# Plain float32 V blocks of the first layer: every sixth block, or 18 blocks beside the last chunk's weights

## The chip, the cores and the metric

The kernel runs on one core of a Trainium2 chip. The metric is device time in microseconds of one launch, given as the median of several runs. The core has a matrix engine (PE, with its weight loads as PEld), a vector engine (DVE), an activation engine (ACT), GpSimd (POOL), a queue engine for transfers (SP), and 16 DMA engines that all queues share.

## What is computed

Two layers of a diffusion backbone over 512 latent tokens and 256 context tokens of width 1024. The part that the change touches is the expert retrieval (PEER) at the end of each layer: every token picks, for 8 heads, the best 16 of 16,384 experts, and

```
act = jax.nn.gelu(jnp.einsum('td,thkd->thk', xb, u_tab[eid]))
return jnp.einsum('thk,thkd->td', gate * act, v_tab[eid])
```

`u_tab` and `v_tab` have 16,384 rows of 1024 float32 each. A token needs 128 rows of each.

## The kernel before

The retrieval is done in two ways at once. For some tiles of 128 tokens the rows that the tokens chose are **gathered**: POOL issues an indirect DMA (L1123) of 128 rows (512 KB) into one of five `grow` buffers, and DVE multiplies it in with one instruction on 128x1024, at L1134 for U (a dot product) and at L1147 for V (an accumulation). In the first layer both context tiles and latent tile 3 are gathered, 128 gathers each for U and V. The other 384 latent tokens go the **dense** way, in `peer_x`: all 128 experts of a block are applied to all 384 tokens, and the activations of experts that a token did not choose are multiplied by zero.

`peer_x` has 128 U blocks and 128 V blocks of 128 experts. A U block loads 512 KB, splits it into a high and a low float32r part, and multiplies it with the tokens in 24 matmuls (tile `pst`); ACT writes the gelu into a slot of the ring `PA`/`PB`, which has R = nA + nB = 64 slots (L1233). A call of `weights(c, i)`, here a round of weights, builds for 8 tokens the gates of one chunk c of blocks from one-hot matrices (DVE: two `o` tiles and `og`; in odd rounds ACT makes the second `o`), multiplies them on PE (16 matmuls, tile `pwt`) and scales the slots by them (DVE, two instructions at L1270). The first layer has three chunks, of 36, 46 and 46 blocks, with 48 rounds each. A V block loads 512 KB into a `uv` tile, of which there are two. A **split** V block then makes `uvh` (ACT, L113) and `uvl` (DVE, L114) from it, and `wh` (ACT) and `wl` (DVE) from the slot, and multiplies in 18 float32r matmuls into the accumulators `dacc`; the `uv` tile is free after the splits. A **plain** V block (the first branch of `vblock`, L1275) has no splits: 6 float32 matmuls, recorded as 12, read the `uv` tile and the slot itself, and the tile is free only after the last of them.

The loop runs m from -nB to 127: the rounds that are due at m, then V block m, then U block m + 64 while there is one. So U ends with m = 63, the second chunk's rounds are due from m = 18 to 35, and the last chunk's from m = 64 to 81. V block 82 is the first to read a slot that the last chunk's rounds scale.

What order the instructions of each engine stand in is settled when the kernel is built: a scheduler gives every engine a fixed list, by the priorities of `prio` (lower numbers first: `peer_x` has 3, the gathers have 6 and fill what the scheduler takes for gaps). On the chip each engine works its list off in order, so a DVE instruction that waits for a gather holds everything behind it. After `peer_x` the second layer's front (L464) follows, which first needs the new latent rows and later those of the context; the last gathers belong to a context tile.

Of the kernel before, what the change touches and what calls it, by code (L numbers as in the profile page):

```python
# [71 lines left out]
class Kern:  # L72
# [101 lines left out]
    def schedule(self):  # L174
        a = self.a
        with ExitStack() as er:
# [19 lines left out]
            with self.banks("x0", "left", w=2, S=2) as ps:  # L196
                with ExitStack() as e:
                    with self.prio(3):
                        pr = e.enter_context(self.banks("x0b", "right", w=2))
                        st = self.front(e, ps, pr, 0, 0, 3, split=False)  # L200
                        ex, keep = ExitStack(), ExitStack()
                        rn = self.back(ps, pr, 0, 0, st, ex, keep=keep)
# [4 lines left out]
                self.gtile_v(0, 1, 0, gc[0])  # L207
                self.gtile_u(0, gc[1])
            with self.prio(3):
                gx, ex = self.peer_x(0, 384, 6, 31, 33, (36, 46, 46), ex, rn)  # L210
            with self.prio(6):
                self.gtile_u(0, gx[3])
                self.gtile_v(0, 0, 3, gx[3])
# [7 lines left out]
                with self.prio(4):  # L221
                    self.back(ps, pr, 1, 0, st, None, (2, 6))
            with self.prio(5):
                gx, _ = self.peer_x(1, 320, 0, 32, 46, (44, 42, 42), (ex,))
            with self.prio(6):
                for i in sorted(gx, reverse=True):
                    self.gtile_u(1, gx[i])
# [953 lines left out]
        nc.sync.dma_start(self.out[t * 128:(t + 1) * 128, :][rows], res[rows])  # L1181


    def peer_x(self, l, T, vn, nA, nB, widths, done, rn=None):

# [5 lines left out]
        R = nA + nB  # L1193
        cuts = [sum(widths[:i]) for i in range(len(widths) + 1)]
        wid = max(widths)
        with ExitStack() as es:
            dn = es.enter_context(self.pool(f"dn{l}"))
            P = [dn.tile([128, nA, T], F32, name="PA")]
# [73 lines left out]

            def vblock(i, sp):
                r0 = l * NEXP + i * 128
                if vn and i % vn == vn - 1:  # L1275
                    raw = dn.tile([128, D], F32, name="uv", bufs=2 + l)
                    nc.sync.dma_start(raw, a["peer_v"][r0:r0 + 128, :])
                    v, w = [raw], [slot(i)]
                else:
                    raw, v = block("v", a["peer_v"][r0:r0 + 128, :])  # L1280
                    w = [sp.tile([128, nd * 128], F32R, name=n, bufs=2) for n in ("wh", "wl")]
                    self.split(*w, slot(i)[:, :nd * 128])
                vh = [[x[:, h * 512:(h + 1) * 512] for x in v] for h in range(2)]
                for t in range(nd):
                    for h in range(2):
                        self.mm([acc[t][:, h * 512:(h + 1) * 512]], [[x[:, t * 128:(t + 1) * 128] for x in w]],
                                [vh[h]], i == 0, i == 127)
                if half:
                    for h in range(2):
                        nc.tensor.matmul(acc[nd][h * 64:(h + 1) * 64], slot(i)[:, nd * 128:T],  # L1290
                                         raw[:, h * 512:(h + 1) * 512], start=(i == 0), stop=(i == 127))
# [174 lines left out]
```

## Time and profile before

| | |
|---|---|
| runs shown, us | 4254.28, 4270.21, 4272.61 (median 4270.21) |
| profiled execution, us | 4259.61, span of its instructions 4257.7 |
| mean granted clock of PE | 0.939 of full speed |
| busy in the span | PE 87%, DVE 82%, PEld 66%, ACT 45%, POOL 36% |
| DMA | 1063.74 MB, mean 250 GB/s |

A share of the span is an average over stages that have different limits. The layer's dense part is therefore cut into stretches below, at instructions that stand in both kernels.

### The profile page before, as it was taken

The page shows a single profiled execution, that of the slowest core. Times are in us where ns is not written, and L with a number is a line of the kernel's source. Part 1 is how long each engine was busy: PE and PEld are TensorE (multiplying, and loading weights), DVE is VectorE, ACT ScalarE, POOL GpSimd, SP SyncE. Part 2 cuts the span into 40 slices and gives each one's busy share as a digit, 9 for nine tenths or more (in the row PEclk, how much of TensorE's full clock was granted, in tenths as well). Part 3 has the DMA queues.
Part 4 walks back from the last instruction along what each step waited for, and adds up shares of the span by engine and source line. Part 5 has one row for each costly group of instructions (what it writes and reads, how often), then busy time and mean ns, then how long its engine had stood idle before and what let it go on. Part 6 is the DMA issues. An engine that isn't in the chain of part 4 may idle for free.

```text
span 4257.7 us, 63783 instructions
## 1 busy us (share of the span) xinstructions
PE 3709.5 (87%) x22514; PEld 2804.8 (66%) x22514; DVE 3508.1 (82%) x7449; ACT 1902.7 (45%) x3719; POOL 1524.0 (36%) x1225
## 2 busy tenths in 40 slices
PE   6887988967989999988968979888888999999997
PEld 3645544557878878877756656447888877776654
DVE  5746988889899989988898875754898988898988
ACT  4555243523247426622552244633334755555732
POOL 0000345642344564366436620000126345553243
PEclk7998998979989999999989989998999999999999
DMA  6655687885768897799879952242359888888697
GB/s 204 203 178 183 214 307 244 300 288 185 250 226 266 307 363 268 243 361 348 292 233 332 348 181 87 84 142 100 138 180 352 270 296 296 294 299 277 227 352 274
DMA packets 305634, 1063.74 MB, mean 250 GB/s; under 512 B 35756, under 2 KB 42624, under 8 KB 305314
## 3 DMA queue, kind: packets, MB, share of 16 engines
q0 software_dynamic: 165888, 604.05, 40.8%
q1 hardware_dynamic: 139426, 455.61, 30.7%
q8 instruction: 177, 2.90, 0.3%
q14 instruction: 143, 1.17, 0.1%
HBM read 1042.69 MB, written 16.84 MB: 249 GB/s over the span
## 4 chain that ended last, share of the span: by engine, by line
PE 32%; DMA 21%; DVE 19%; issue 16%; POOL 6%; ACT 5%; SPq 0%; POOLq 0%; DVEq 0%; ACTq 0%
PE pst L121 7%; POOL grow L1123 6%; PE dacc L121 6%; DMA grow<-in_peer_u_dram,eid 6%; DMA grow<-in_peer_v_dram,eid 5%; DMA uv<-in_peer_v_dram 4%; PE pwin L121 4%; DMA uv<-in_peer_ut_dram 3%; DVE uvl L114 3%; DVE acc L1147 3%; DVE acc L1134 2%; PE ppq L121 2%; DMA wmod<-in_w_mod_dram 2%; PE pwo L121 1%; PE fp L414 1%
## 5 line engine op out<-in xcount | busy, mean ns | idle before, releaser
L1123 POOL DMA_INDIRECT grow<-in_peer_u_dram,eid x576 | 749.6, 1301 | 1166.6 <-DVE acc L1134 591.8
L1123 POOL DMA_INDIRECT grow<-in_peer_v_dram,eid x576 | 766.8, 1331 | 748.0 <-DVE acc L1147 604.4
L121 PE MATMUL pst<-dhT,uvh 128*128 128x384 f32 (+1 forms) x4096 | 998.6, 328 | 0.0
L113 ACT CAST uvh<-uv 128x1024 fp32r<-128x1024 f32 x491 | 512.9, 1045 | 699.7 <-DMA uv<-in_peer_v_dram 422.4
L121 PE MATMUL pst<-dhT,uvl 128*128 128x384 f32 (+1 forms) x2048 | 695.2, 339 | 115.5 <-DVE uvl L114 83.9
L1147 DVE SCALAR_TENSOR_TENSOR acc<-grow,gate,acc 128x1024 f32<-128x1024 f32 x571 | 732.9, 1283 | 49.9 <-DMA grow<-in_peer_v_dram,eid 42.9
L1134 DVE SCALAR_TENSOR_TENSOR acc<-grow,ghx 128x1024 f32<-128x1024 f32 x576 | 704.4, 1223 | 73.4 <-DMA grow<-in_peer_u_dram,eid 68.4
L121 PEld LDWEIGHTS pst<-dhT,uvh 128*128 128x128 f32 x4096 | 730.6, 192 | 2.8 <-issue 1.2
L114 DVE TENSOR_TENSOR uvl<-uv,uvh 128x1024 fp32r<-128x1024 f32 x491 | 599.5, 1222 | 154.8 <-ACT uvh L113 152.1
L121 PEld LDWEIGHTS pst<-dhT,uvl 128*128 128x128 f32 x2048 | 394.2, 192 | 218.2 <-DVE uvl L114 163.5
L121 PE MATMUL dacc<-uvh,wl 128*128 128x512 f32 x1154 | 482.0, 418 | 40.1 <-ACT uvh L113 21.3
L121 PE MATMUL dacc<-uvl,wh 128*128 128x512 f32 x1154 | 468.8, 406 | 25.7 <-DVE uvl L114 25.4
L121 PE MATMUL dacc<-uvh,wh 128*128 128x512 f32 x1154 | 462.9, 401 | 0.0
L1263 ACT ACTIVATE o<-iota,di2n 128x128 f16<-128x128 f16 x1056 | 325.2, 389 | 27.6 <-PE pwt L1267 27.4
L121 PEld LDWEIGHTS dacc<-uvh,wl 128*128 128x128 f32 x1154 | 220.6, 191 | 130.3 <-ACT uvh L113 37.0
L121 PEld LDWEIGHTS dacc<-uvl,wh 128*128 128x128 f32 x1154 | 221.1, 192 | 84.5 <-DVE uvl L114 40.2
L121 PEld LDWEIGHTS dacc<-uvh,wh 128*128 128x128 f32 x1154 | 221.2, 192 | 47.9
L1267 PEld LDWEIGHTS <-o 128*128 128x128 f16 x4224 | 126.4, 97 | 104.3 <-issue 31.1
L1233 ACT ACTIVATE PA<-pst 128x320 f32<-128x320 f32 (+1 forms) x126 | 58.4, 463 | 290.4 <-PE pst L121 290.3
L1267 PE MATMUL pwt<-og,o 128*128 128x46 f16 (+3 forms) x4224 | 152.3, 183 | 37.1 <-DVE og L1253 29.7
L1233 ACT ACTIVATE PB<-pst 128x384 f32<-128x384 f32 (+1 forms) x130 | 60.0, 462 | 218.2 <-PE pst L121 218.1
L256 POOL MEMSET rmod<- 128x512 f32 (+1 forms) x8 | 3.3, 416 | 421.1 <-PE ptmod L282 171.8
(403 smaller groups left out, 6104.5 us busy)
## 6 DMA issues: line engine op xcount, KB each, us to landing
uv<-in_peer_ut_dram SPq DMA_DIRECT2D x256, 512.0 KB
uv<-in_peer_v_dram SPq DMA_DIRECT2D x256, 512.0 KB
wmod<-in_w_mod_dram SPq DMA_DIRECT2D x96, 512.0 KB
wpq<-in_peer_wq_dram SPq DMA_DIRECT2D x48, 512.0 KB
w_in<-in_w_in_dram SPq DMA_DIRECT2D x72, 256.0 KB
w_in<-in_w_in_dram SPq DMA_DIRECT2D x18, 512.0 KB
grow<-in_peer_u_dram,eid POOLq DMA_INDIRECT x576, 6.6
grow<-in_peer_v_dram,eid POOLq DMA_INDIRECT x576, 6.8
```

Of the source, the lines that this page charges most:

```text
L113: self.nc.scalar.copy(hi, src)
L114: self.nc.vector.tensor_tensor(lo, src, hi.bitcast(F32), op=ALU.subtract)
L121: self.nc.tensor.matmul(p, w[i], x[j], start=start and n == 0, stop=stop and n == len(passes) - 1)
L256: nc.gpsimd.memset(r, 0.0)
L414: self.nc.tensor.matmul(p, w, x, start=(i == 0), stop=(i == len(pairs) - 1))
L1123: self.nc.gpsimd.indirect_dma_start(out=r, out_offset=None, in_=self.a[table], in_offset=bass.IndirectOffsetOnAxis(ap=eid[:, j:j + 1], axi ...
L1134: nc.vector.scalar_tensor_tensor(junk, r, 1.0, hx, op0=ALU.mult, op1=ALU.mult, accum_out=dot[:, j:j + 1])
L1147: nc.vector.scalar_tensor_tensor(acc, r, w[:, j:j + 1], acc, op0=ALU.mult, op1=ALU.add)
L1233: nc.scalar.activation(slot(i), p, AF.Gelu_apprx_tanh)
L1263: nc.scalar.activation(o2[:, q], self.iota, AF.Abs, bias=i2n[:, t, k * NC + q:k * NC + q + 1])
L1267: nc.tensor.matmul(p[:, q, :], o2[:, q, :], og[:, g, q, :], start=(g == 0), stop=(g == 1))
```

## The change

The argument vn (every vn-th V block plain) goes; in the first layer the plain blocks are now those from 128 - R to the start of the last chunk, which is 64 to 81: 18 blocks in a row. Before they were 5, 11, ... 125: 21 blocks. The second layer had none and has none.

```diff
-                gx, ex = self.peer_x(0, 384, 6, 31, 33, (36, 46, 46), ex, rn)
+                gx, ex = self.peer_x(0, 384, 31, 33, (36, 46, 46), ex, rn)
...
-                gx, _ = self.peer_x(1, 320, 0, 32, 46, (44, 42, 42), (ex,))
+                gx, _ = self.peer_x(1, 320, 32, 46, (44, 42, 42), (ex,))
...
-    def peer_x(self, l, T, vn, nA, nB, widths, done, rn=None):
+    def peer_x(self, l, T, nA, nB, widths, done, rn=None):
...
         wid = max(widths)
+
+        plain = range(128 - R, cuts[-2]) if l == 0 else ()
...
             def vblock(i, sp):
                 r0 = l * NEXP + i * 128
-                if vn and i % vn == vn - 1:
+                if i in plain:
```

The lists of the engines move with it. POOL's list of gathers keeps its order. On DVE they stand elsewhere between the other instructions. Here is DVE's list early among the last chunk's rounds (V blocks 64 to 81), before: `og`, `o` and the two at L1270 belong to the rounds, `uvl` and `wl` to split V blocks, L1147 is a gather.

```order
L1253 TENSOR_TENSOR og<-o_18387,diT 128x736
L1147 SCALAR_TENSOR_TENSOR acc<-grow,gate,acc 128x1024
L1270 SCALAR_TENSOR_TENSOR PA<-pwt,PA 128x13x8
L1270 SCALAR_TENSOR_TENSOR PB<-pwt,PB 128x33x8
L1248 TENSOR_TENSOR o_18448<-iota,diT 128x368
L1259 TENSOR_TENSOR o_18510<-iota,diT 128x1024
L1253 TENSOR_TENSOR og<-o_18448,diT 128x736
L114 TENSOR_TENSOR uvl<-uv,uvh 128x1024
L1270 SCALAR_TENSOR_TENSOR PA<-pwt,PA 128x13x8
L1270 SCALAR_TENSOR_TENSOR PB<-pwt,PB 128x33x8
L1248 TENSOR_TENSOR o_18473<-iota,diT 128x368
L114 TENSOR_TENSOR wl<-PA,wh 128x384
```

The same place of the changed kernel:

```order
L1255 TENSOR_TENSOR og<-o_18567,diT 128x736
L1147 SCALAR_TENSOR_TENSOR acc<-grow,gate,acc 128x1024
L1272 SCALAR_TENSOR_TENSOR PA<-pwt,PA 128x13x8
L1272 SCALAR_TENSOR_TENSOR PB<-pwt,PB 128x33x8
L1250 TENSOR_TENSOR o_18608<-iota,diT 128x368
L1261 TENSOR_TENSOR o_18670<-iota,diT 128x1024
L1255 TENSOR_TENSOR og<-o_18608,diT 128x736
L1147 SCALAR_TENSOR_TENSOR acc<-grow,gate,acc 128x1024
L1272 SCALAR_TENSOR_TENSOR PA<-pwt,PA 128x13x8
L1272 SCALAR_TENSOR_TENSOR PB<-pwt,PB 128x33x8
L1250 TENSOR_TENSOR o_18633<-iota,diT 128x368
L1147 SCALAR_TENSOR_TENSOR acc<-grow,gate,acc 128x1024
```

Where `uvl` and `wl` stood, there are now gathers. The second place is DVE's list just behind the last round, where V block 82 begins, before (x2 and so on: equal instructions in a row):

```order
L114 TENSOR_TENSOR wl<-PA,wh 128x384 x2
L1147 SCALAR_TENSOR_TENSOR acc<-grow,gate,acc 128x1024 x4
L114 TENSOR_TENSOR uvl<-uv,uvh 128x1024
L114 TENSOR_TENSOR wl<-PA,wh 128x384
L1147 SCALAR_TENSOR_TENSOR acc<-grow,gate,acc 128x1024 x6
L114 TENSOR_TENSOR uvl<-uv,uvh 128x1024
L114 TENSOR_TENSOR wl<-PA,wh 128x384
L1147 SCALAR_TENSOR_TENSOR acc<-grow,gate,acc 128x1024 x2
```

and in the changed kernel:

```order
L114 TENSOR_TENSOR wl<-PA,wh 128x384 x2
L1147 SCALAR_TENSOR_TENSOR acc<-grow,gate,acc 128x1024 x4
L114 TENSOR_TENSOR uvl<-uv,uvh 128x1024
L114 TENSOR_TENSOR wl<-PA,wh 128x384
L1147 SCALAR_TENSOR_TENSOR acc<-grow,gate,acc 128x1024 x2
L114 TENSOR_TENSOR uvl<-uv,uvh 128x1024
L114 TENSOR_TENSOR wl<-PA,wh 128x384
L1147 SCALAR_TENSOR_TENSOR acc<-grow,gate,acc 128x1024 x2
```

Two gathers now stand between any two V blocks; before there were 4 to 6 around a plain one. The third place is DVE's list where the last gathers meet the second layer's front (`hT`, `xn`, `w_inl`, `hc` are the front's, L1156 and L1172 end the gathered context tile), before:

```order
L1147 SCALAR_TENSOR_TENSOR acc<-grow,gate,acc 128x1024
L114 TENSOR_TENSOR hT_22355<-hraw,hT_22354 128x4x128 x2
L107 SCALAR_TENSOR_TENSOR nrt<-nry,nrm 128x1
L1156 TENSOR_TENSOR acc<-acc,grow 128x1024
L108 SCALAR_TENSOR_TENSOR nry<-nrt,nry 128x1
L1172 TENSOR_TENSOR grow<-grow,acc 128x1024
L423 TENSOR_SCALAR xn<-xr,nry 128x1024
L114 TENSOR_TENSOR w_inl<-w_in,w_inh 128x512
```

and in the changed kernel:

```order
L1147 SCALAR_TENSOR_TENSOR acc<-grow,gate,acc 128x1024
L114 TENSOR_TENSOR hT_22415<-hraw,hT_22414 128x4x128 x2
L107 SCALAR_TENSOR_TENSOR nrt<-nry,nrm 128x1
L1147 SCALAR_TENSOR_TENSOR acc<-grow,gate,acc 128x1024
L108 SCALAR_TENSOR_TENSOR nry<-nrt,nry 128x1
L1147 SCALAR_TENSOR_TENSOR acc<-grow,gate,acc 128x1024
L423 TENSOR_SCALAR xn<-xr,nry 128x1024
L1147 SCALAR_TENSOR_TENSOR acc<-grow,gate,acc 128x1024
L114 TENSOR_TENSOR w_inl<-w_in,w_inh 128x512
```

Ten gathers more stand behind the dense part than before. Counted over the whole list of DVE between instructions that both kernels have, the gathers (L1134 and L1147), the splits `uvl` and `wl`, and the rounds (`og`) move as follows. S1 runs from the first `wl` to the 51st `og` of the layer (the first of the second chunk behind two that stand ahead), S2 from there to the 98th, S3 to the 99th, S4 to the 144th and last, S5 to the first instruction that reads `dacc` (L1332), S6 to the last gather of the context tile.

| stretch | V blocks, about | gathers before, after | `uvl` | `wl` | `og` |
|---|---|---|---|---|---|
| S1 | 0 to 19 | 90, 83 | 33, 36 | 16, 19 | 1, 1 |
| S2 | 20 to 36 | 42, 36 | 32, 35 | 14, 17 | 47, 47 |
| S3 | 37 to 63 | 135, 129 | 53, 56 | 25, 27 | 1, 1 |
| S4 | 64 to 81 | 30, 56 | 16, 2 | 13, 0 | 45, 45 |
| S5 | 82 to 127 | 111, 94 | 36, 44 | 38, 46 | 0, 0 |
| S6 | behind V | 16, 26 | 0, 0 | 0, 0 | 0, 0 |

On SP the loads keep their order; three small transfers for the end of the layer (`PA<-rows`, two `PA<-xsd`) stand one or two V loads earlier. Behind the front of the second layer the lists are the same.

## Rows read from the trace of the kernel before

**Rows 1.** The page's busy times: engine, busy us, share of the span, instructions.

```profile
PE 3709.5 (87%) x22514; PEld 2804.8 (66%) x22514; DVE 3508.1 (82%) x7449; ACT 1902.7 (45%) x3719; POOL 1524.0 (36%) x1225
```

**Rows 2.** Windows S1 to S6: PE, PEld, DVE, ACT, POOL busy; clock, DMA share, GB/s.

```profile
1433.50:1619.60 186.10, 169.67 (x792) 139.18 (x790) 157.06 (x237) 54.23 (x79) 122.59 (x90) 0.97 0.97 356
1619.60:1790.40 170.80, 169.81 (x1438) 143.11 (x1439) 165.20 (x342) 122.25 (x269) 57.60 (x43) 1.00 0.73 240
1790.40:2077.50 287.10, 258.89 (x1217) 214.24 (x1216) 243.89 (x261) 81.25 (x114) 182.14 (x136) 0.98 0.95 351
2077.50:2216.00 138.50, 105.39 (x1022) 75.49 (x1020) 132.95 (x265) 98.42 (x231) 29.62 (x31) 0.88 0.67 216
2216.00:2456.10 240.10, 214.69 (x795) 150.87 (x796) 200.16 (x189) 54.22 (x74) 148.92 (x112) 0.96 0.93 336
2456.10:2495.50 39.40, 10.01 (x38) 7.06 (x37) 39.26 (x65) 21.79 (x50) 15.38 (x17) 0.53 0.80 277
```

**Rows 3.** L1147 in S5, and L1134 in S1: count, shortest, median, longest ns.

```profile
L1147 DVE SCALAR_TENSOR_TENSOR acc<-grow,gate,acc x111: 1272/1285/1341, 2216.5 to 2454.9; 128x1024 f32<-128x1024 f32 x111
...
L1134 DVE SCALAR_TENSOR_TENSOR acc<-grow,ghx x90: 1217/1224/1228, 1435.3 to 1617.4; 128x1024 f32<-128x1024 f32 x90
```

**Rows 4.** PE's timeline around a plain block of S5: start, us, instruction, count.

```profile
2254.81 5.31 PE L121 MATMUL dacc<-uv,PA 128*128 128x512 f32 x12
...
2260.42 0.40 PE L121 MATMUL dacc<-uvh,wh 128*128 128x512 f32 x1
...
2263.94 0.40 PE L121 MATMUL dacc<-uvh,wh 128*128 128x512 f32 x1
```

**Rows 5.** DVE's timeline late in S4: two rounds and three gathers.

```profile
2190.65 0.54 DVE L1253 TENSOR_TENSOR og<-o,diT 128x736 f16<-128x736 f16 x1
2191.11 1.28 DVE L1147 SCALAR_TENSOR_TENSOR acc<-grow,gate,acc 128x1024 f32<-128x1024 f32 x1
2192.30 0.26 DVE L1270 SCALAR_TENSOR_TENSOR PA<-pwt,PA 128x104 f32<-128x104 f32 x1
...
2194.13 1.28 DVE L1147 SCALAR_TENSOR_TENSOR acc<-grow,gate,acc 128x1024 f32<-128x1024 f32 x1
2195.32 0.26 DVE L1270 SCALAR_TENSOR_TENSOR PA<-pwt,PA 128x104 f32<-128x104 f32 x1
...
2197.29 0.54 DVE L1253 TENSOR_TENSOR og<-o,diT 128x736 f16<-128x736 f16 x1
```

**Rows 6.** DVE's timeline in S5: a split V block between gathers.

```profile
2340.30 1.21 DVE L114 TENSOR_TENSOR uvl<-uv,uvh 128x1024 fp32r<-128x1024 f32 x1
2341.43 0.55 DVE L114 TENSOR_TENSOR wl<-PB,wh 128x384 fp32r<-128x384 f32 x1
2341.90 2.60 DVE L1147 SCALAR_TENSOR_TENSOR acc<-grow,gate,acc 128x1024 f32<-128x1024 f32 x2
```

**Rows 7.** Windows of S4 in two parts, and the first of S5, as in 2.

```profile
2077.50:2182.00 104.50, 97.74 (x862) 68.97 (x860) 98.98 (x202) 79.87 (x185) 17.24 (x19) 0.98 0.65 212
2182.00:2216.00 34.00, 7.64 (x161) 6.52 (x160) 33.97 (x64) 18.55 (x46) 12.38 (x12) 0.55 0.72 229
2216.00:2223.00 7.00, 3.80 (x23) 3.12 (x24) 6.49 (x10) 0.92 (x2) 4.24 (x4) 0.50 0.91 289
```

**Rows 8.** SP's and ACT's timelines in S1: a V load and its cast.

```profile
1484.51 0.33 SPq L1224 DMA_DIRECT2D uv<-in_peer_v_dram  x1
...
1490.11 1.04 ACT L113 CAST uvh<-uv 128x1024 fp32r<-128x1024 f32 x1 [6.49 <-DMA uv<-in_peer_v_dram]
```

**Rows 9.** Waits in S5: who for whom, us in all, times, longest us.

```profile
ACT uvh L113 <- DMA uv<-in_peer_v_dram: 145.0, 32, 8.8
```

**Rows 10.** Window behind S6, the second layer's front, as in 2.

```profile
2495.50:2530.00 34.50, 34.50 (x145) 28.43 (x144) 21.40 (x36) 10.79 (x20) 0.67 (x10) 0.94 0.34 109
```

## The prediction

> **What bounds the kernel now.** The page is read first [rows 1]: PE 87% and DVE 82% busy, no engine full, which says only that the stages differ. So the dense part of the first layer is cut into windows S1 to S6, at DVE instructions that both kernels have [rows 2]. The reader is to see that two kinds of stretch alternate. In S1, S3 and S5 the DMA engines are the full ones: share 0.97, 0.95 and 0.93 at 356, 351 and 336 GB/s, while PE and DVE are busy for 83 to 91% of the time. In S2 it is PE (169.8 of 170.8 us) and in S4 DVE (133.0 of 138.5 us), and there the DMA engines move only 240 and 216 GB/s. S6 is DVE again (39.3 of 39.4 us).
>
> That S1, S3 and S5 are paced by bytes can be checked by counting. One block load and one gather are both 512 KB, 0.524 MB. S1 moves 356 GB/s x 186.1 us = 66.3 MB, that is 126 transfers, and by the table of the change it holds 90 gathers and about 36 block loads. S3 moves 100.8 MB = 192 transfers (135 gathers, some 56 loads), S5 80.7 MB = 154 (111 gathers, some 43 loads). The gathers' counts in the trace are those of the list [rows 3]. So in these three stretches a gather costs its bytes: 0.524 MB / 0.356 = 1.47 us in S1, 1.49 in S3, 1.56 in S5, whatever it costs DVE.
>
> **The prices of the engines.** A plain block is 12 records in 5.31 us. The split block behind it has a matmul every (2263.94 - 2260.42)/15 = 0.235 us, so 18 of them take 17 x 0.235 + 0.40 = 4.39 us, both counted to the end of the last one [rows 4]. Plain costs PE 0.92 us more. On DVE the two rounds and three gathers from 2190.65 to 2197.29 take 6.64 us without a gap; a gather holds the engine 2192.30 - 2191.11 = 1.19 us, so a round takes (6.64 - 3.57)/2 = 1.53 us on average [rows 5]. A split block's `uvl` takes 2341.43 - 2340.30 = 1.13 us and its `wl` 0.47 [rows 6]: plain spares DVE 1.60 us.
>
> **The change part by part.** Three plain blocks fewer save PE 2.8 us and cost DVE 4.8 us in all, which is little. What counts is where the list now puts 424 gathers that are the same in number: 36 leave S1 to S3 and S5 (7, 6, 6 and 17), 26 of them go into S4 and 10 into S6.
>
> S1 loses 7 gathers: 7 x 1.47 = 10 us. Cover for more isn't there: PE is at 91%, and three splits more on DVE (4.8 us) stand against seven gathers less (8.3 us). If DMA did not pace it, the gain is PE's three plain blocks alone, 2.8 us; that is one bound, and 13 us with the DMA share at 1.0 the other. I take -10.
>
> S2 is PE's own: three plain blocks become split, 3 x 0.92 = 2.8 us; the 6 gathers that leave cost nothing there. -3, between 0 and -6 (DVE, at 97%, loses 7.1 us and gains 4.8).
>
> S3 loses 6 gathers, 9 us by bytes, between 3.7 us (four plain blocks on PE) and 13. I take -9.
>
> S4 is where the splits go and the gathers come. By the prices it held 45 x 1.53 + 30 x 1.19 + 16 x 1.13 + 13 x 0.47 = 128.7 us of DVE work in 138.5 us, 93%. In the new list it is 45 x 1.53 + 56 x 1.19 + 2 x 1.13 = 137.8 us; at the same 93% that is 148 us, +10. The 24 us that the splits spare are more than spent by 26 gathers (31 us). There is less air than before, though. In the part up to the last plain block (the first window) PE was busy 97.7 of 104.5 us [rows 7]; 15 blocks at 0.92 us make it 111.5 us of the 114 that DVE takes there (148 less the 34 of the second window), and a round goes from DVE to PE and back, with about three plain matmuls queued ahead of it on PE. Each hitch on one engine then reaches the other. I take +14, between +4 (DVE without a gap) and +30. The loads don't set it: from issue to cast a V load took 5.6 us at a DMA share of 0.97 [rows 8]; with two tiles, each held for a load and for a block of 5.3 us and its rounds' matmuls, a block could come about every 6 us, and DVE lets one through every 114/18 = 6.3. On ACT 15 casts of `uvh` and `wh` go, and it wasn't full (98 of 138.5 us).
>
> S5 gets 8 splits more and 17 gathers less. DVE's balance is 8 x 1.60 - 17 x 1.19 = -7 us, PE's 8 x -0.92 = -7 us, so both stay under the end; the bytes fall by 8.9 MB, at the rate held 26 us. The bounds: 15 us if the turn-around of the two `uv` tiles rather than bytes sets part of it (ACT's casts wait 145 us in all for V loads there [rows 9]), 38 us if the stretch came up to the 356 GB/s of S1. I take -26.
>
> On this the Trainium skill has a rule (DMA: Bandwidth & Descriptors, section "Where 436 GB/s comes from"): transfers from HBM to SBUF are bound at about 358 GB/s for each core. S1's 356 and S3's 351 GB/s [rows 2] agree with it. By that figure S5 would take (80.7 - 8.9) MB / 0.358 = 201 us, 39 less, and the sum would be 13 us lower than mine; an estimate from that page, which I do not use as the end of a range.
>
> S6 and what follows: ten gathers more stand among the first matmuls of the second layer. They are 10 x 1.19 = 12 us of DVE work, and the first 34.5 us there left DVE 13.1 us idle while PE was busy throughout [rows 10]. Most of it hides; a `w_inl` that stands behind a late gather holds PE. +3, between 0 and +10. SP's list moves three small transfers by one or two V loads, each behind blocks that the two `uv` tiles make it wait for anyway: nothing. From there on the lists are equal, so the rest keeps its time.
>
> **Sum.** -10 - 3 - 9 + 14 - 26 + 3 = -31 us. Against the profiled execution of 4259.6 us that is 4228.6. That execution lies 10.6 us under the median of the runs shown, and the four executions have their middle at 4264.9; from there the sum gives 4234, and that is my number.
>
> **The rivals.** *S4 eats it.* Plain blocks, rounds and gathers need 97% of PE and 93% of DVE at once in the first window. If the two lose a tenth to each other, S4 costs +30 and S5, with its tiles turning slowly, gives only 20: -9 in all, 4256, no change that can be told. For it speaks how close the two sums lie; against it that DVE kept 93% with PE at 94% already [rows 7]. Chance 0.27, with the milder mixtures of it.
>
> *S5 fills up.* With plain blocks gone the loads come evenly, and S5 reaches S1's 356 GB/s: 38 us in place of 26, 4222. S5 is the stretch with the most room below S1's rate. Chance 0.18.
>
> *PE slows down in S4.* The granted clock was 0.98 while PE was 94% busy, and 0.55 in the 34 us in which DVE alone worked off the last rounds; V block 82 then began at 0.50, the 1.2 GHz level [rows 7]. In the new list PE waits before each round's matmuls. If these waits took the clock to 1.2 GHz for the whole of the first window, 111.5 us of PE work become 223, S4 grows by some 110 us and the kernel by 65, to 4330. It decides from about half of that window at 1.2 GHz: 4234 + 55 lies near 0.5% above the old median. Against it: PE would be about as busy there as it was, and slow matmuls fill its gaps themselves. Chance 0.05. The Trainium skill (TensorE: Matmul & The Clock Gate, section "What's actually happening") has the low level as the default, released by activity; that goes with the 0.55 and 0.50 of the rows, and it is the rule by which this case would come.
>
> *The change does nothing of this* is excluded by the lists: the gathers stand where the table says.
>
> **How the numbers follow.** The forecast itself, -20 to -50 us, has 0.50; with the others that makes 1. The limit of what counts as a change, 0.5% of 4270, is 21 us, about what a measurement of this kernel can tell from none. The forecast and a full S5 make it faster, less a tenth of the forecast that lies near the limit: 0.63. S4's case and that tenth make no change: 0.32. The clock's case is the slower one: 0.05. The ends of the terms add up to -66 and +19 us, which no case reaches with all terms at once; eight in ten lie between -59 and -5 from the 4265, so 4206 to 4260.
>
> **What the profile will show.** Right: S1, S3 and S5 shorter by 10, 9 and 26 us at rates within 2 or 3% of before, S4 at about 152 us with DVE still over 93% busy and DMA up from 216 towards 290 GB/s, the front of the second layer with PE hardly waiting. Wrong: S4 over 165 us, with rounds on DVE waiting for `pwt` or gathers; S5 above 225 us, or its GB/s below 320; S1 or S3 unchanged although their gathers left; a clock under 0.9 in the first 100 us of S4.

## The result, and the profile after

The changed kernel takes 4217.44 us (median of six runs, 4202.68 to 4229.7), the kernel before 4271.41 us beside it (six runs): a ratio of 0.9876, 95% interval 0.9848 to 0.9904, that is 41 to 65 us less. The profiled execution of the changed kernel is the longest of its six, 4229.7 us, and 30 us shorter than that of before.

The page's busy line, as in [rows 1], tells as little as before:

```profile
PE 3702.5 (88%) x22532; PEld 2806.4 (66%) x22532; DVE 3509.9 (83%) x7455; ACT 1908.9 (45%) x3725; POOL 1543.7 (37%) x1225
```

The windows S1 to S6 of the changed kernel answer to [rows 2] (PE, PEld, DVE, ACT, POOL busy; clock, DMA share, GB/s). The last row is a stretch that is needed below, called the end: from the first read of `dacc` to the last matmul into `pwin`, a tile of the second layer's front. Behind it the lists are the same.

```profile
1431.45:1607.30 175.85, 162.36 (x808) 138.58 (x807) 152.92 (x229) 58.29 (x85) 122.12 (x83) 1.00 0.96 358
1607.30:1776.40 169.10, 168.49 (x1456) 147.49 (x1457) 162.83 (x335) 125.68 (x276) 48.44 (x37) 0.99 0.69 226
1776.40:2051.50 275.10, 252.81 (x1244) 216.06 (x1242) 239.97 (x272) 88.28 (x123) 177.26 (x129) 1.00 0.96 353
2051.50:2197.80 146.30, 117.06 (x928) 60.48 (x928) 142.19 (x264) 79.02 (x200) 56.90 (x57) 0.88 0.86 301
2197.80:2409.40 211.60, 199.65 (x836) 155.00 (x837) 191.38 (x189) 65.29 (x90) 142.93 (x94) 0.98 0.94 337
2409.40:2473.10 63.70, 34.84 (x137) 26.71 (x136) 61.88 (x92) 27.69 (x60) 31.38 (x33) 0.71 0.82 276
2409.40:2580.30 170.90, 135.88 (x634) 110.92 (x632) 103.89 (x162) 64.68 (x133) 32.55 (x47) 0.87 0.46 149
```

The end of the kernel before:

```profile
2456.10:2622.30 166.20, 131.81 (x626) 109.08 (x625) 92.70 (x152) 64.70 (x133) 16.95 (x37) 0.87 0.37 123
```

S1, S3 and S5 are shorter by 10.2, 12.0 and 28.5 us at rates of 358, 353 and 337 GB/s (356, 351 and 336 before), S2 by 1.7. S4 is 7.8 us longer with DVE at 97%, the end 4.7. To the last `pwin` matmul that makes 42 us (2622.3 - 2580.3). The rest of the kernel took 1635.4 us before and 1647.6 now (spans 4257.7 and 4227.9), although its lists are the same. One of the experiments (x_some_before) has the lists of before and took 1654.0 there (4269.6 - 2449.1 - 166.5): this part scatters by 10 to 20 us between executions, and so the two profiles differ by only 30 us, where the medians show 54.

S4 in parts, as in [rows 7]:

```profile
2051.50:2155.00 103.50, 101.03 (x705) 49.86 (x706) 99.61 (x187) 56.05 (x144) 41.58 (x42) 0.98 0.88 313
2155.00:2197.80 42.80, 16.03 (x224) 10.62 (x222) 42.58 (x78) 22.97 (x56) 15.32 (x16) 0.62 0.82 273
2197.80:2205.00 7.20, 3.99 (x24) 3.23 (x25) 7.13 (x11) 0.92 (x2) 4.76 (x4) 0.50 0.83 270
```

In the first 103.5 us PE is busy for 97.6% and DVE for 96.2% at a clock of 0.98. In S5 the waits of [rows 9] read

```profile
ACT uvh L113 <- DMA uv<-in_peer_v_dram: 114.8, 36, 5.5
```

Four waits more than before, but 30 us less in all, and the longest is 5.5 us in place of 8.8.

### The profile page after: what moved, and what is told of

It reads as the page before. It is cut to its first block, busy times and chain, and to the rows that moved or that the text cites. A ratio compares the mean times of both kernels' runs of the same rounds, so it can differ in the third digit from the quotient of the medians.

```text
span 4227.9 us, 63819 instructions
## 1 busy us (share of the span) xinstructions
PE 3702.5 (88%) x22532; PEld 2806.4 (66%) x22532; DVE 3509.9 (83%) x7455; ACT 1908.9 (45%) x3725; POOL 1543.7 (37%) x1225
## 4 chain that ended last, share of the span: by engine, by line
PE 35%; DMA 21%; DVE 18%; issue 15%; POOL 7%; ACT 5%; SPq 0%; POOLq 0%; DVEq 0%; ACTq 0%
PE pst L121 8%; PE dacc L121 7%; DMA grow<-in_peer_u_dram,eid 7%; POOL grow L1123 7%; DMA uv<-in_peer_v_dram 5%; PE pwin L121 4%; DMA uv<-in_peer_ut_dram 3%; DMA grow<-in_peer_v_dram,eid 3%; DVE uvl L114 2%; PE ppq L121 2%; DVE acc L1147 2%; DVE acc L1134 2%; PE fp L414 2%; PE pwo L121 2%; DMA wmod<-in_w_mod_dram 2%
## 5 line engine op out<-in xcount | busy, mean ns | idle before, releaser
L1123 POOL DMA_INDIRECT grow<-in_peer_v_dram,eid x576 | 782.1, 1358 | 700.5 <-DVE acc L1147 553.8
L1134 DVE SCALAR_TENSOR_TENSOR acc<-grow,ghx 128x1024 f32<-128x1024 f32 x576 | 703.1, 1221 | 76.1 <-DMA grow<-in_peer_u_dram,eid 71.1
L1147 DVE SCALAR_TENSOR_TENSOR acc<-grow,gate,acc 128x1024 f32<-128x1024 f32 x571 | 731.1, 1280 | 33.5 <-DMA grow<-in_peer_v_dram,eid 27.0
L256 POOL MEMSET rmod<- 128x512 f32 (+1 forms) x8 | 3.3, 417 | 419.3 <-PE ptmod L282 169.2
```

What stands on the lines that cost most here:

```text
L256: nc.gpsimd.memset(r, 0.0)
L1123: self.nc.gpsimd.indirect_dma_start(out=r, out_offset=None, in_=self.a[table], in_offset=bass.IndirectOffsetOnAxis(ap=eid[:, j:j + 1], axi ...
L1134: nc.vector.scalar_tensor_tensor(junk, r, 1.0, hx, op0=ALU.mult, op1=ALU.mult, accum_out=dot[:, j:j + 1])
L1147: nc.vector.scalar_tensor_tensor(acc, r, w[:, j:j + 1], acc, op0=ALU.mult, op1=ALU.add)
```

## The experiments

**Theory 1** is the prediction's: S1, S3 and S5 are paced by bytes, and the gain is that gathers leave them for S4. **Theory 2**, the rival: the plain blocks themselves cost time in S1, S3 and S5, and the gain is that they left. From the fifth run on it has a sharper form: a plain block keeps one of the two `uv` tiles through its 5.3 us of matmuls. All edits are to the changed kernel unless said otherwise; each run was timed beside the kernel before.

The stretches of all profiled executions, us, and the medians, with the median of before in the same comparison:

| kernel | S1 | S2 | S3 | S4 | S5 | end | median | before | ratio (95%) |
|---|---|---|---|---|---|---|---|---|---|
| before | 186.1 | 170.8 | 287.1 | 138.5 | 240.1 | 166.2 | | | |
| changed | 175.9 | 169.1 | 275.1 | 146.3 | 211.6 | 170.9 | 4217.4 | 4271.4 | 0.9876 (0.9848 to 0.9904) |
| x_none | 174.1 | 167.5 | 273.3 | 128.0 | 214.9 | 213.9 | 4250.5 | 4271.2 | 0.9944 (0.9921 to 0.9967) |
| x_both | 187.2 | 169.7 | 294.7 | 150.7 | 237.1 | 156.1 | 4264.4 | 4271.2 | 0.9984 (0.9968 to 1.0001) |
| x_small_before | 158.5 | 169.6 | 248.3 | 136.0 | 205.3 | 166.6 | 4099.8 | 4271.2 | 0.9597 (0.9579 to 0.9616) |
| x_small_after | 155.1 | 168.0 | 242.7 | 140.3 | 197.2 | 169.0 | 4090.1 | 4271.2 | 0.9573 (0.9551 to 0.9596) |
| x_some_before | 182.1 | 170.9 | 289.7 | 139.1 | 237.1 | 166.5 | 4268.0 | 4275.2 | 0.9982 (0.9961 to 1.0003) |
| x_some_after | 169.2 | 167.6 | 270.9 | 147.6 | 207.6 | 169.9 | 4222.1 | 4275.2 | 0.9875 (0.9846 to 0.9904) |
| x_s3 | 174.0 | 167.5 | 322.6 | 129.2 | 212.7 | 173.7 | 4247.0 | 4275.2 | 0.9927 (0.9902 to 0.9951) |
| x_s2s4 | 171.5 | 210.5 | 271.8 | 150.9 | 211.1 | 157.0 | 4245.7 | 4275.2 | 0.9924 (0.9901 to 0.9947) |
| x_hold | 179.9 | 172.3 | 283.8 | 149.2 | 230.2 | 169.3 | 4259.6 | 4265.4 | 0.9980 (0.9962 to 0.9999) |
| x_pe | 176.5 | 172.0 | 270.7 | 152.3 | 219.6 | 167.0 | 4228.0 | 4265.4 | 0.9904 (0.9880 to 0.9928) |
| x_own | 186.0 | 169.9 | 287.6 | 139.3 | 235.3 | 167.3 | 4266.9 | 4265.4 | 0.9995 (0.9978 to 1.0012) |
| x_own_s5 | 172.5 | 167.6 | 277.2 | 150.9 | 235.1 | 166.4 | 4237.0 | 4265.4 | 0.9921 (0.9895 to 0.9946) |

Stretches of kernels with the same lists there differ by up to 5 us (S1 is 171.5 to 175.9 in the changed kernel, x_s2s4 and x_own_s5, S4 146.3 to 150.9 in the changed kernel, x_some_after and x_own_s5), so a difference of that size in one stretch tells nothing.

### x_none and x_both: the change's two halves

```diff
# x_none
-        plain = range(128 - R, cuts[-2]) if l == 0 else ()
+        plain = () if l == 0 else ()
# x_both
-        plain = range(128 - R, cuts[-2]) if l == 0 else ()
+        plain = (*range(128 - R, cuts[-2]), *range(5, 64, 6), *range(83, 128, 6)) if l == 0 else ()
```

Expected of x_none: 

> No plain block at all. Theory 1 (the gain is gathers that leave the byte-bound S1, S3 and S5 for room that the plain blocks open in S4): in this kernel's list S4 holds 22 gathers (56 in the changed kernel), S3 127 (129), S5 91 (94), and 65 stand behind the V blocks in S6 (26). Against the 4217 us of the changed kernel: S4 -14 us (124 us of DVE work in place of 138, at the same 0.94 busy), S3 -3, S5 -5, and 39 more gathers in S6 cost between +18 us (0.47 us each, as the ten of the change did) and +57 us (their bytes): 4213 to 4252, middle 4233; S1 and S5 keep the lengths that they have in the changed kernel. Theory 2 (the gain is the removal of plain blocks from S1, S3 and S5 itself, by PE's 0.92 us and the uv tile's longer hold; the 18 beside the weights add nothing): 4200 or less, since S4 gives its 14 us back and nothing is lost.

Expected of x_both: 

> The old sixth blocks outside 64 to 81 stay plain, and 64 to 81 are plain too: 36 plain blocks. Theory 1: S4 holds 56 gathers, S5 99 (before 111), S3 137 (135), S6 none (16). Against the kernel before: S4 +8 us as in the changed kernel, S5 12 x 1.56 = -19, S3 +3, S6 and the second layer's front 16 x 0.47 = -7: about -15 us, 4256, with S1 as long as before (186 us). Theory 2: no plain block has left S1, S3 or S5, so nothing is gained and S4 costs 8 us more: 4279.

The removal alone gave 21 us, the addition alone 7 (its interval, 14 to 0 us, reaches none at all), the two together 54. x_none's S1, its S4 and S5, and its end (as two answers of the windows):

```profile
1445.94:1620.05 174.11, 161.06 (x808) 138.25 (x807) 153.09 (x229) 57.12 (x80) 119.50 (x84) 1.00 0.96 357
...
2060.84:2188.85 128.01, 100.86 (x1035) 77.16 (x1035) 125.01 (x260) 102.54 (x241) 20.17 (x22) 0.89 0.57 190
2188.85:2403.75 214.90, 201.21 (x836) 154.88 (x837) 191.25 (x188) 65.28 (x90) 134.69 (x92) 0.98 0.93 333
...
2403.75:2617.70 213.95, 138.72 (x634) 111.86 (x632) 151.77 (x201) 66.26 (x134) 88.57 (x86) 0.81 0.63 215
```

Without any plain block S1, S3 and S5 are about as short as in the changed kernel (174, 273, 215), so what stands in S4 has no part in their gain. But 65 gathers now stand behind the V blocks, and the end takes 213.9 us. The 18 plain blocks beside the weights take 34 of these gathers into S4: S4 18 us longer, the end 43 shorter. That is their part in the change; the median is near the upper end of what theory 1 expected (4213 to 4252), since S5 gave back nothing and the end cost 1.10 us a gather. Theory 2 had asked for 4200 or less: it misses by 50 us, as it had left out the gathers at the end.

x_both's windows of S1, S3 and S5:

```profile
1422.71:1609.87 187.16, 168.73 (x791) 137.69 (x790) 157.46 (x238) 54.47 (x79) 123.38 (x90) 0.98 0.96 353
...
1779.58:2074.32 294.74, 263.94 (x1217) 218.95 (x1215) 244.73 (x260) 81.10 (x114) 185.70 (x138) 0.96 0.94 347
...
2224.99:2462.12 237.13, 214.31 (x785) 151.68 (x786) 187.65 (x180) 54.33 (x74) 126.66 (x99) 0.94 0.87 313
```

Here theory 1 misses. S5 holds 12 gathers fewer than before, and it is only 3 us shorter, not 19: the rate fell to 313 GB/s instead. With its plain blocks in place, S5 did not get shorter by having less to move. Theory 2's number, 4279, is missed as well: the end got 10 us shorter.

### x_small_before and x_small_after: nearly all bytes of the gathers gone

The edit to both kernels, for the first layer; it changes nothing in DVE's work and hardly the lists.

```diff
-        self.nc.gpsimd.indirect_dma_start(out=r, out_offset=None, in_=self.a[table],
+        self.nc.gpsimd.indirect_dma_start(out=r[:, 0:64] if l == 0 else r, out_offset=None,
+            in_=self.a[table].rearrange("r (a b) -> (r a) b", b=64) if l == 0 else self.a[table],
...
+        if l == 0:
+            return r[:, 0:64].unsqueeze(1).to_broadcast([128, 16, 64])
```

Expected of x_small_before: 

> The kernel before, with gathers of the first layer that fetch 64 of each row's 1024 numbers (DVE multiplies these 64 sixteen times over, so it works as long as before; the gathered tiles' results are not the reference's). DVE's list holds 90, 42, 136, 31, 111 and 12 gathers in S1 to S6. Theory 1: the bytes are gone, so S1, S3 and S5 fall to the engines' work, some 172, 262 and 217 us (now 186, 287 and 240); S2 and S4 as before. In all 60 us or more below the kernel before. Theory 2: plain blocks hold S1, S3 and S5 up, so these shorten by little, 20 us together at most.

Expected of x_small_after: 

> The changed kernel with the same small gathers of the first layer (same part left out). DVE's list holds 83, 36, 129, 54, 94 and 26 gathers in S1 to S6, nearly as in the changed kernel. Against x_small_before, theory 1: S1, S3 and S5 differ only by the engines' prices, -3, -4 and -7 us, S2 -3, S4 +8, S6 and the front +5: about -4 us (between -15 and +10) where the full kernels differ by 54. Theory 2: the difference is that of the full kernels, 40 us or more.

S1 and S5 of x_small_before:

```profile
1374.95:1533.48 158.53, 158.53 (x789) 136.94 (x789) 155.89 (x237) 51.88 (x76) 121.43 (x90) 1.00 0.44 142
...
2087.38:2292.65 205.27, 202.09 (x787) 147.62 (x788) 199.97 (x190) 54.99 (x74) 148.88 (x112) 0.98 0.38 126
```

and of x_small_after:

```profile
1372.40:1527.46 155.06, 155.06 (x804) 139.75 (x804) 152.42 (x230) 54.85 (x79) 117.93 (x83) 1.00 0.44 143
...
2078.51:2275.70 197.19, 194.01 (x833) 156.05 (x834) 193.38 (x188) 65.36 (x90) 132.86 (x94) 0.98 0.39 128
```

Both fall by more than theory 1 asked for, and PE fills S1 to the last (158.53 of 158.53 us). The difference between the two kernels shrinks from 54 us to 10, and by stretches to -3.5, -1.6, -5.5, +4.3, -8.1 and +2.4: the engines' prices, as expected (-3, -3, -4, +8, -7, +5). So the gain needs traffic, and theory 2 in its first form fails: it had asked for 20 us at most in x_small_before, and for a difference of 40 or more. It does not follow that each gather is paid by its bytes, and the next pair shows that it isn't.

### x_some_before and x_some_after: the bytes of 30 gathers gone

The same edit for 30 numbered gathers, 7 in S1, 6 in S3 and 17 in S5, in both kernels; every list stays as it was.

```diff
+        self.count = getattr(self, "count", -1) + 1
+        small = self.count in (*range(345, 424, 13), *range(480, 586, 21), *range(648, 729, 5))
```

Expected of x_some_before: 

> The kernel before with every list unchanged, but 30 of its gathers small (64 of 1024 numbers of each row; the rest of what these fetch is left out): 7 in S1, 6 in S3, 17 in S5, as many as the change took out of each stretch. DVE works as before; only 0.49 MB each of traffic goes. Theory 1 (bytes pace S1, S3 and S5): -10, -8 and -25 us, 4228. Theory 2 (the plain blocks that hold the two uv tiles pace S5, and partly S1 and S3; x_both had 12 gathers less in S5 than the kernel before and gained 3 us there): -3, -2 and -5 us, 4261.

Expected of x_some_after: 

> The changed kernel with the same 30 small gathers (same part left out), lists unchanged. Theory 1: -10, -8 and -25 us here too, 4174. Theory 2: with no plain block in S1, S3 and S5 the loads come evenly and the bytes pace them fully, so the same 4174; only x_some_before tells the two apart. If S1, S3 and S5 stood at the floor of their engines, it would be 4210 or more.

S1, S3 and S5 of x_some_before, to be held against [rows 2]:

```profile
1430.17:1612.30 182.13, 165.53 (x791) 135.51 (x790) 157.32 (x238) 54.00 (x79) 122.94 (x90) 1.00 0.94 344
...
1783.21:2072.87 289.66, 261.97 (x1217) 216.62 (x1216) 244.19 (x261) 80.80 (x114) 178.65 (x136) 0.97 0.93 337
...
2211.97:2449.11 237.14, 214.12 (x795) 152.18 (x796) 200.12 (x189) 54.33 (x74) 150.25 (x112) 0.95 0.88 304
```

-4.0, +2.6 and -3.0 us, and 7 us in the median (interval -17 to +1) where theory 1 asked for 43. The stretches kept their length and the rate fell, to 304 GB/s in S5. This settles it against theory 1's price in the kernel before, by S3, S5 and the sum (S1's -4.0 is no larger than the scatter). In the changed kernel it is little better: -6.7, -4.2 and -4.0 us in the profile, about 0.5 us a gather, and nothing that the median can tell (4222.1; both theories had said 4174). So in S5 a DMA share of 0.94 at 337 GB/s does not make bytes the price of a transfer there either. In S1 and S3 alone, where bytes asked for 10 and 8 us, the scatter leaves it open. The floor of the engines that this run's expectation names (4210 or more) fits the median, though PE was still idle for some 9 us each of S1 and S5.

### x_s3 and x_s2s4: the plain blocks at other places

```diff
# x_s3
+        plain = range(44, 62) if l == 0 else ()
# x_s2s4
+        plain = (*range(20, 36), *range(64, 82)) if l == 0 else ()
```

Expected of x_s3: 

> 18 plain blocks in a row as in the changed kernel, but V blocks 44 to 61, in S3. The list then holds 156 gathers in S3 (129 in the changed kernel), 22 in S4 (56), 92 in S5 (94), 35 in S6 (26). If the place matters: S3 +27 x 1.47 = +40 us, S4 -18 as in the kernel without plain blocks, S5 -3, S6 9 x 1.10 = +10: about 4246. If only the number of plain blocks matters, and that U ends or not does not: 4217.

Expected of x_s2s4: 

> The rule of the change applied to both chunks: plain in 64 to 81 and also in 20 to 35, beside the second chunk's rounds. S2 holds 73 gathers (36), S3 127 (129), S5 86 (94), S6 none (26). S2: PE 169 + 16 x 0.92 = 184 us, DVE 47 x 1.53 + 73 x 1.19 + 20 x 1.13 = 181 us, so +17 us if one of them is full, +26 at 94%. S3 -3, S5 8 x 1.5 = -12, the end of the dense part -15 as in x_both. Theory 1: -13 to -4, 4204 to 4213. The rival, that PE and DVE lose to each other in S2, where U blocks also need both: S2 +40 and more, 4227.

S3 of x_s3, then S2 and S5 of x_s2s4:

```profile
1785.14:2107.77 322.63, 285.62 (x1138) 205.28 (x1136) 248.17 (x267) 59.66 (x82) 201.98 (x156) 0.94 0.94 344
```

```profile
1605.50:1815.97 210.47, 193.71 (x1377) 135.57 (x1378) 182.49 (x379) 107.98 (x249) 91.20 (x74) 0.96 0.80 276
...
2238.73:2449.78 211.05, 198.92 (x833) 154.40 (x834) 184.15 (x182) 65.29 (x90) 123.33 (x86) 0.98 0.89 320
```

x_s3 came out at 4247.0, as expected for "the place matters": 18 plain blocks in S3, and the 29 gathers that the list moves there with them, make it 49 us longer than x_none's: 2.7 us a block, three times PE's 0.92. The number had been added up with the bytes' price (27 x 1.47 us), so that it was met says nothing for the hold; and it was met in sum only (S3 +47.5 us against 40 over the changed kernel, the end +2.8 against 10). x_s2s4 went beyond its rival (4227). S2 grew by 41 us with neither PE (92%) nor DVE (87%) full: plain blocks cost far beyond PE's price there too, where U blocks use the same two tiles, at only 276 GB/s. And S5, with eight gathers fewer than in the changed kernel, is 0.5 us shorter, where 12 were expected.

### x_hold and x_pe: what of a plain block costs

18 split blocks (those of the old sixth places outside S4) get one thing each that a plain block has: x_hold a last reader of the `uv` tile behind their matmuls, x_pe about 0.94 us more of matmuls. `zero` is a tile of zeros.

```diff
# x_hold
+                if l == 0 and i % 6 == 5 and i not in plain:
+                    nc.tensor.matmul(acc[0][:, 0:64], zero, raw[:, 0:64], start=False, stop=False)
# x_pe
+                if l == 0 and i % 6 == 5 and i not in plain:
+                    for t in range(4):
+                        nc.tensor.matmul(acc[t % 3][:, 0:512], zero, v[0][:, 0:512], start=False, stop=False)
```

Expected of x_hold: 

> The changed kernel, in which the 18 split blocks that were plain before outside 64 to 81 end with one more small matmul (64 columns of the uv tile times zeros, which adds nothing): their uv tile is held until their matmuls end, as a plain block's is, while the splits and nearly all of the list stay (83, 38, 130, 53, 96, 24 gathers). Theory 2 in its sharper form (the hold of one of the two uv tiles, while loads take long beside the gathers, costs the time): S1, S3 and S5 lengthen by what x_both has over the changed kernel, less PE's 0.92 us for a block: +8, +16 and +18 us, 4259. If the hold costs nothing: the small matmuls alone, at most 6 us in all, 4221.

Expected of x_pe: 

> The changed kernel, in which the same 18 split blocks get four more float32r matmuls (0.235 us each, zeros times uvh, nothing added): PE's price of a plain block without the hold and without the spared splits. Gathers by the list: 85, 39, 130, 56, 100, 17. If PE sets S1 to S5: 18 x 0.94 = +17 us, and -4 for nine gathers fewer at the end, 4230. If PE only fills waits for loads there: 4215. If PE's load is what made plain blocks cost in S1, S3 and S5 (what x_both has over the changed kernel there, 56 us), about 4260.

S1, S3 and S5 of x_hold, and of x_pe:

```profile
1436.24:1616.12 179.88, 163.49 (x807) 141.20 (x807) 153.06 (x230) 55.77 (x77) 120.64 (x84) 0.97 0.95 352
...
1788.43:2072.25 283.82, 254.33 (x1240) 218.58 (x1239) 240.13 (x270) 86.78 (x121) 179.11 (x131) 0.98 0.95 346
...
2221.44:2451.65 230.21, 208.03 (x853) 161.30 (x854) 193.71 (x190) 66.06 (x90) 138.46 (x96) 0.95 0.90 318
```

```profile
1429.05:1605.51 176.46, 163.22 (x817) 140.28 (x816) 155.21 (x234) 57.36 (x80) 121.96 (x86) 1.00 0.97 359
...
1777.47:2048.17 270.70, 251.71 (x1246) 217.22 (x1245) 239.70 (x269) 85.29 (x116) 186.24 (x131) 1.00 0.96 358
...
2200.44:2420.01 219.57, 207.16 (x869) 160.88 (x870) 198.65 (x195) 66.13 (x90) 144.87 (x100) 0.98 0.94 339
```

x_hold lands on its median, 4259.6. Its small matmul has little part in that, as PE's timeline in S5 shows:

```profile
2262.88 0.33 PE L1293 MATMUL dacc<-uv,zero 128*128 128x64 f32 x2
2263.02 0.48 PE L121 MATMUL dacc<-uvh,wl 128*128 128x512 f32 x1
2263.34 0.40 PE L121 MATMUL dacc<-uvl,wh 128*128 128x512 f32 x1
```

From its start to that of the second matmul behind it are 2263.34 - 2262.88 = 0.46 us, 0.23 more than from one of a block's matmuls to the next: 4 us for 18 blocks. So it is the hold that takes back most of the 42 us between the changed kernel and x_hold (4217.4 and 4259.6); by stretches these are 4.0, 8.7 and 18.6 us in S1, S3 and S5.

x_pe has more work on PE than x_hold, 17 us for 18 blocks, and no hold: 4228.0, as PE's price asked for (4230). Against x_pe, x_hold is longer by 3.4, 13.1 and 10.6 us in S1, S3 and S5, and by 32 us in the median. That is the least that the hold is worth here. It comes with a lower rate and a lower granted clock (0.97, 0.98 and 0.95, in x_pe 1.00, 1.00 and 0.98). PE's work alone costs nothing that can be told in S1 and S3 (+0.6 and -4.4 against the changed kernel), and in S5 its own price, 8.0 us for eight blocks. Two limits: in x_hold the tile is held through the splits as well, so a plain block's hold need not cost quite the same; and x_pe's S4 is 6.0 us longer than the changed kernel's with the same 56 gathers, which is open.

The timeline of the kernel before shows the hold at work, at V block 113 of S5 (start, us, engine, instruction, and in brackets the idle time before and who ended it):

```profile
2380.81 5.31 PE L121 MATMUL dacc<-uv,PB 128*128 128x512 f32 x12
...
2382.80 1.04 ACT L113 CAST uvh<-uv 128x1024 fp32r<-128x1024 f32 x1 [5.61 <-DMA uv<-in_peer_v_dram]
...
2383.87 1.23 DVE L114 TENSOR_TENSOR uvl<-uv,uvh 128x1024 fp32r<-128x1024 f32 x1 [3.25 <-ACT uvh L113]
...
2385.13 1.35 SPq L1224 DMA_DIRECT2D uv<-in_peer_v_dram  x2
...
2385.48 5.24 DVE L1147 SCALAR_TENSOR_TENSOR acc<-grow,gate,acc 128x1024 f32<-128x1024 f32 x4
...
2389.71 1.05 ACT L113 CAST uvh<-uv 128x1024 fp32r<-128x1024 f32 x1 [5.45 <-DMA uv<-in_peer_v_dram]
...
2390.81 0.50 PE L121 MATMUL dacc<-uvh,wl 128*128 128x512 f32 x1 [0.47 <-ACT uvh L113]
```

The plain block holds one tile until 2386.12. The other has block 114's data from before 2382.80. So no V load is on its way until 2385.13, when `uvl` of 114 is done; the second of the two loads in the SP row goes out at its end, 2386.15 (the row spans 1.35 us, an issue takes 0.33 [rows 8]), when the plain matmuls are done. The first is cast 4.6 us after its issue, and PE, which had run through block 114 meanwhile, waits 0.47 us for its `uvh`.

### x_own and x_own_s5: plain blocks that hold no tile

The eight plain blocks of S5 load into ring slots that nobody needs any more (x_own changes the kernel before).

```diff
+                    k = {83: 0, 89: 3, 95: 22, 101: 25, 107: 28, 113: 22, 119: 25, 125: 28}.get(i)
+                    if k is None:
+                        raw = dn.tile([128, D], F32, name="uv", bufs=2 + l)
+                    else:
+                        raw = free[:, k * T:k * T + D]
# x_own_s5 as well
+        plain = (*range(128 - R, cuts[-2]), *range(83, 128, 6)) if l == 0 else ()
```

Expected of x_own: 

> The kernel before, in which the eight plain blocks of S5 load into ring slots that are used up, so that they hold neither uv tile; gathers 90, 42, 135, 30, 110, 17, plain blocks and splits as before. Theory 2, the hold: S5 from 240 to about 222 us, 4253. If gathers or PE's work set S5: unchanged, 4271.

Expected of x_own_s5: 

> The changed kernel with the eight plain blocks of S5 back, loading into used-up ring slots. The list puts 110 gathers into S5 (94) and 10 into S6 (26). Theory 2, the hold: S5 211.6 + 7.4 (PE) + 16 gathers at about 0.25 us = 223 us, the end of the dense part 16 x 0.47 to 16 x 1.10 shorter, -8 to -18: 4217 give or take 6. If 16 gathers cost their bytes in S5, 1.5 us each, 4235.

Both miss: 235.3 us in S5 where the hold asked for 222, no difference in x_own's median, and 4237.0 in place of 4217. Both come out at the number that stood against the hold: unchanged for x_own, and for x_own_s5 the 4235 of gathers that cost their bytes (S5 235.1 us, at the changed kernel's rate of 337 GB/s). x_own's waits in S5 show that the tiles did turn faster, and what came instead:

```profile
ACT uvh L113 <- PE dacc L121: 99.9, 21, 8.4
ACT uvh L113 <- DMA uv<-in_peer_v_dram: 69.5, 15, 9.3
...
PEld dacc L121 <- DVE wl L114: 26.5, 12, 4.4
DVE acc L1147 <- DMA grow<-in_peer_v_dram,eid: 26.2, 27, 2.8
```

ACT waits half as long for V loads as in [rows 9], since they come early now; but DVE waits for gathers, and PE for DVE. DVE's waits for gathers in S5 were shorter in the kernel before,

```profile
DVE acc L1147 <- DMA grow<-in_peer_v_dram,eid: 11.9, 15, 2.5
```

and nearly nothing in the changed kernel:

```profile
DVE acc L1147 <- DMA grow<-in_peer_v_dram,eid: 0.7, 3, 0.3
```

x_own's DVE timeline at block 122, three behind the plain block 119:

```profile
2423.20 5.24 DVE L1147 SCALAR_TENSOR_TENSOR acc<-grow,gate,acc 128x1024 f32<-128x1024 f32 x4
2429.89 1.28 DVE L1147 SCALAR_TENSOR_TENSOR acc<-grow,gate,acc 128x1024 f32<-128x1024 f32 x1 [1.45 <-DMA grow<-in_peer_v_dram,eid]
2431.53 1.28 DVE L1147 SCALAR_TENSOR_TENSOR acc<-grow,gate,acc 128x1024 f32<-128x1024 f32 x1 [0.35 <-DMA grow<-in_peer_v_dram,eid]
2432.73 1.22 DVE L114 TENSOR_TENSOR uvl<-uv,uvh 128x1024 fp32r<-128x1024 f32 x1
```

Six gathers stand in a row in DVE's list there. The fifth and sixth had not landed; `uvl` of block 122, which stands behind them, starts at 2432.73, and PE's next matmul waits 2.83 us for DVE. The wait is followed by a low clock: PE then works for 2.6 us at a granted 0.52, near its 1.2 GHz level, its matmuls 0.43 us apart in place of 0.235 (window as in [rows 2]).

```profile
2434.40:2437.00 2.60, 2.53 (x6) 2.07 (x7) 2.56 (x4) 0.00 (x0) 1.47 (x2) 0.52 0.89 326
```

But the edit did a second thing: it lengthened the bunches of gathers. Between two `uvl` of S5 the trace of the kernel before has six gathers only twice, at the first plain block, and otherwise mostly two to four (the x4 in the timeline above is one such place); x_own's and x_own_s5's have six eight times and otherwise two, the changed kernel's two almost throughout. The 4 to 6 around a plain block that the section on the change gives hold for the first one only. So this pair took the hold away and brought longer bunches, and it does not tell what the hold costs in the kernel before. What it shows is that S5 stays long without the hold when its gathers stand so. Nor does it tell the bunches from the number of gathers, 110 in place of 94, which came with them; that each is paid by its bytes is what the numbered gathers (x_some_before, x_some_after) speak against. For the hold, x_hold is the test: its lists have at most three gathers in a row behind the first plain block's place.

## Why the prediction was right, and where it wasn't

**The sum.** -31 us was forecast; the profile shows -42 to the end of what the change moves, the medians -54. By terms: S1 -10 (measured -10.2), S2 -3 (-1.7), S3 -9 (-12.0), S4 +14 (+7.8), S5 -26 (-28.5), S6 and the front +3 (+4.7). The medians' 54 lie a little beyond the 20 to 50 us of the forecast, and within the 4206 to 4260 given for eight cases in ten.

**The step that failed** is the one under S1, S3 and S5: "in these three stretches a gather costs its bytes". The sizes came out nearly as forecast, but by luck. The count that was to show it can't: a stretch's rate times its length gives its transfers whatever paces it, in S2 too (240 GB/s x 170.8 us = 41.0 MB = 78 transfers, 42 gathers and 35 block loads), which PE sets. Taking away the bytes of as many gathers as the change removed gave -4.0, +2.6 and -3.0 us with the lists untouched (x_some_before), and 12 gathers fewer in S5 gave -3 (x_both). What cost most of the time were the plain blocks: the held tile (x_hold) and in S5 PE's 0.92 us (x_pe). That their bunched gathers cost something is argued from x_own's waits and not shown by itself. That PE and DVE were busy for only 83 to 91% in these stretches was read as a sign that DMA sets them; in S5 it was a chain of waits, in which the loads took long because of the traffic (with small gathers S5 of the kernel before fell to 205.3 us). The bound that pointed the right way was the lower one of S5 ("if the turn-around of the two `uv` tiles rather than bytes sets part of it"). The signs that the prediction named for being right nearly all came, down to rates within 1% of before; none of them could tell bytes from a held tile.

How S5's 28.5 us divide is known in part. PE was busy for 15.0 us less (214.7 to 199.7) and idle for 13.5 us less. Of the whole, 7.4 is PE's price (8 x 0.92). The hold by itself is worth 16.7 (x_hold over the changed kernel, 18.6, less 8 x 0.23 for the small matmuls), or at least 10.6 (x_hold over x_pe). If these add up, 4 to 11 us are left for the bunches and for the 17 gathers that left, which no kernel here separates. S3's 12.0 us go with the hold too (8.7 of x_hold, 13.1 over x_pe). In S1 x_hold gives back 4.0 of the 10.2 us, and the bytes of seven gathers gave 4.0 and 6.7; all three are within or near the scatter, so what set S1 stays open.

**S2 and the engines' prices** held: x_small_after against x_small_before shows them with the traffic gone.

**S4** was over-priced. DVE was busy for 142.2 of 146.3 us (137.8 by the count of prices); I took 93% and four us more for PE and DVE losing time to each other, and they lost little: both were over 96% busy in the first 103.5 us. (With the same list there x_own_s5 took 150.9 us, so the term was too large by 2 to 6 us.) So the rival that S4 eats the gain was wrong, and the one of the clock too (0.98 in that window). S5 did not fill up either (337 GB/s); that 4217 lies nearer to that rival's 4222 than to 4234 says nothing for it. Two smaller sums of the prediction are off and move no term: by its own counts the splits spare 14 x 1.13 + 13 x 0.47 = 21.9 us in S4, not 24, and S1 at a DMA share of 1.0 would be 186.1 - (66.3 - 3.7) / (0.356 / 0.97) = 15.5 us shorter, not 13.

**S6** and the front cost 0.47 us a gather for ten more, within the bounds of their term. x_none shows the price further out: 39 gathers more cost 43 us, 1.10 each. That is what the plain blocks beside the weights save, and the prediction did not see it, since it compared S4 with the kernel before and not with none: the two halves of the change are worth little alone (21 and 7 us), because removal pushes gathers to the end, and S4's blocks take them back where the rounds already pace PE and DVE.

**What the list said, and what not.** The counts of the list were right to the gather. The forecast put a price on each count and took the counts as the cause; the list had also moved the pattern, from three or four gathers in a row around a plain block (six around the first) to two between any two V blocks. Of the kernels that do all the work, none tried beats the changed one.

## What to carry to other kernels

A stretch at 0.93 of the DMA engines, as S5, need not be priced by bytes, and multiplying its rate by its length can't tell: make some transfers small with every list kept, and see whether it gets shorter. A block that spares splits but keeps its load buffer until its matmuls end costs buffer turns, which no busy share shows; with two buffers, put such blocks where the loads have time. Here S4 was such a place; S2, which PE paces but where U blocks turn the same two tiles, was not (x_s2s4). When an edit takes one cost away, compare the lists again: x_own's edit brought another. And when removing and adding are one change, run both halves: here neither is the gain.

## What the runs showed of the hardware

The traffic never went above 362 GB/s in a stretch (S1 of x_s2s4). The Trainium skill (DMA: Bandwidth & Descriptors, section "Where 436 GB/s comes from") gives about 358 GB/s as what binds a core's transfers between HBM and SBUF. The rows of whole stretches agree with it to about 1% (362, and 359 in x_pe's S1); in slices of 6 us the rate of x_own's S5 goes up to 414. S5 of the kernel before, at 336 GB/s, lost a tenth of its rate (304 in x_some_before) and was only 3 us shorter.

A gather of a sixteenth of the bytes landed in half the time, not in a sixteenth, although the traffic beside it was also lower (126 GB/s in place of 336). These are the issues of gathers in S5 of the kernel before and of x_small_before (count, median us from issue to landing):

```profile
grow<-in_peer_v_dram,eid POOLq DMA_INDIRECT x112, 7.1
```

```profile
grow<-in_peer_v_dram,eid POOLq DMA_INDIRECT x112, 3.4
```

A float32 matmul of 64 columns between float32r matmuls of 512 cost PE 0.23 us in x_hold, as much as one more of those (0.235).

After 2.8 us without work PE's granted clock was 0.52 for the next 2.6 us in x_own, so that wait was paid a second time by the matmuls behind it.
